# Query columns of the dilated attention units copied side by side on GpSimd

## The chip, the cores and the metric

One Trainium2 chip, one of its cores. The metric is the device time of one execution in microseconds. A core has five engines with queues of their own that work in order: TensorE (PE, matmuls, with its weight loads shown apart as PEld), VectorE (DVE), ScalarE (ACT), GpSimd (POOL) and SyncE (SP, which here only issues transfers).

## What is computed

One layer of a decoder trunk on x (2048 tokens, 1024 wide, float32): a norm, a projection, two token mixers side by side (a gated delta rule with four heads of 128, and a dilated sliding-window attention with eight heads of 64), an output projection, a norm, a gated MLP of width 2816 with a short convolution, and a last norm. The change lies in the dilated attention:

```python
DILATED_CONFIGS = ((128, 1), (512, 4), (2048, 16))      # window, dilation
for window, dilation in DILATED_CONFIGS:
    # tokens of equal residue modulo the dilation form a sequence of their own;
    # each of its blocks of 128 queries attends its own and the previous block
    sub = lambda t: t.reshape(bn, l, dilation, h, dh).transpose(0, 2, 3, 1, 4).reshape(bn * dilation, h, l, dh)
    o, lse = banded_causal_attention(sub(q), sub(k), sub(v), window // dilation, dilation, slopes)
    ...
weights = jax.nn.softmax(jnp.stack(lses), axis=0)
return jnp.einsum('gbsh,gbshd->bshd', weights, jnp.stack(outs))
```

## The kernel before

The program runs in stages: a projection (phase_p), the two mixers together (phase_mix, where gdn_rec is the delta rule and class Swa the attention), and the output projection and MLP (phase_e). phase_mix interleaves the steps of both mixers in one program; the framework's scheduler then fixes the order of each engine's queue before the program runs, and every wait is a semaphore.

An attention head has its queries and keys in SBUF with the features on the partitions and the 2048 tokens along the free dimension, as float32 split into two parts that PE takes at full rate: q2 holds both parts of q on 64 partitions each, k1 and k2 hold the two parts of k twice. load_qk brings the next head's three tiles while this one is worked on.

Swa.units lists 48 units of 128 queries in 19 groups: groups 0 to 7 are the near units (dilation 1, d = 0), groups 8 to 14 the 16 units of dilation 4 (d = 1; the four of group 8 have 128 keys, the other twelve 256, two units a group), groups 15 to 18 the 16 units of dilation 16 (d = 2, 128 keys, four units a group). Swa.cols (L563) takes a unit's columns from q2 or k1/k2: 128 or 256 neighbouring columns for d = 0, every fourth for d = 1, every sixteenth for d = 2. So the dilated units' columns lie 16 and 64 bytes apart.

Swa.scores (L600) goes through the groups. Each unit takes two products into one PSUM tile, q2 with k1 (L625) and q2 with k2 (L627); the query columns are the loaded weights, the key columns are streamed. VectorE then adds the bias and takes the row maximum (L632). At group 15 GpSimd spreads the maxima (spread, L664, L667), PE and VectorE gather them (L675, L677, L679), and after group 18 the common maximum of the three dilations goes back the same way.

Swa.values follows some 21 groups behind, so head h's values are worked on beside head h+1's scores: exponentials (L694), transposes on PE (L701), their copy by ScalarE (L704), the product with v (L722), and its sum into acc (L729, L735). Swa.divide (L740) is run in small steps beside the values of the next head: it stores the denominators, loads them reshaped, inverts and stores them, loads each quarter broadcast over 64 partitions (rb, L762, on SyncE's queue), multiplies on GpSimd (L769) and stores the quarter from ScalarE's queue (L771). The last head's division uses other buffers and engines. rb comes from a pool whose tiles have two buffers each unless told otherwise.

GpSimd's other work in this stage: block copies of the delta rule (L413, L414), its row scalings (L497 to L501), the attention's bias tiles (L548), and the spreading above.

Of the kernel before, what the change touches and what calls it, by code (L numbers as in the profile page):

```python
# [9 lines left out]
F32 = mybir.dt.float32  # L10
F32R = mybir.dt.float32r
# [7 lines left out]
P = 128  # L19
# [4 lines left out]
NB = T // 512  # L24
# [493 lines left out]
class Swa:  # L518
# [44 lines left out]
    def cols(self, t, d, u, prev, rows):  # L563
# [5 lines left out]
            return t[rows, :].rearrange("p (j r) -> p j r", r=4)[:, (u[0] + 1 - w) * P:(u[0] + 1) * P, u[1]]  # L569
        return t[rows, :].rearrange("p (j r) -> p j r", r=16)[:, :, u]  # L570

    def load_v(self, h):
        nc, n = self.n.nc, self.n
        src = n.sv[h // 4][T * (h % 4):T * (h % 4) + T, :]
        v = self.v[h % 2]
        nc.sync.dma_start(v[:, 32:48, :], src.rearrange("(p r) f -> p r f", r=16))
        for b in range(4):
            nc.sync.dma_start(v[:, 16 + 4 * b:20 + 4 * b, :],
                              src[512 * b:512 * b + 512, :].rearrange("(p r) f -> p r f", r=4))
        nc.sync.dma_start(v[:, 0:16, :], src.rearrange("(b p) f -> p b f", p=P))  # L580
# [19 lines left out]
    def scores(self, h):  # L600
        n = self.n
        nc, v = n.nc, n.nc.vector
        load = self.load_qk(h + 1, nc.sync, 2) if h + 1 < SH else iter(())
        q2, k1, k2 = self.loaded.pop(h)
        m = self.wk.tile([P, 48], F32, tag="m", name="m")
        nm = self.wk.tile([P, 48], F32, tag="nm", name="nm")
        mt = self.wk.tile([P, 32], F32, tag="mt", name="mt")
        tiles = []
        full = slice(0, P)
        for gi, (d, us) in enumerate(self.units()):  # L610
            if gi:
                next(load, None)
            if gi == 2 and h:
                self.slopes(h, (2,))
            if gi in (8, 15) and h + 1 < SH:
                self.slopes(h + 1, (gi // 15,))
            ps = n.bank(tag="sc")
            slot = self.free.pop(0)
            s = self.sp.tile([P, 512], F32, tag=f"s{slot}", name="s")
            o, rs = 0, []  # L620
            for col, u, prev in us:
                w = 256 if prev else P
                rs.append(slice(o, o + w))
                r = ps[:, o:o + w]
                nc.tensor.matmul(r, self.cols(q2, d, u, False, full), self.cols(k1, d, u, prev, full),  # L625
                                 start=True, stop=False)
                nc.tensor.matmul(r, self.cols(q2, d, u, False, full), self.cols(k2, d, u, prev, full),  # L627
                                 start=False, stop=True)
                o += w
            for (col, u, prev), r in zip(us, rs):  # L630
                bo = P if d < 2 and not prev else 0
                n.mark = v.tensor_tensor_reduce(out=s[:, r], in0=ps[:, r], in1=self.bias[d][:, bo:bo + r.stop - r.start], scale=1.0,  # L632
                                       scalar=-3e38, op0=ALU.add, op1=ALU.max, accum_out=m[:, col:col + 1])
            tiles.append((slot, s))
            if gi == 15:
                lay = self.spread(m[:, 0:32], 0)
            if gi == 17:
                self.gather(mt, lay, 0)
            yield None

        x = nm[:, 32:48]
        v.tensor_tensor(x, m[:, 32:48], mt[:, 0:16], op=ALU.max)
        v.tensor_tensor(x, x, mt[:, 16:32], op=ALU.max)
        v.tensor_scalar(x, x, -1.0, None, op0=ALU.mult)
        back = self.spread(x, 1)
        self.later = [lambda: self.gather(nm, back, 1)]
        yield tiles, nm
# [92 lines left out]
    def divide(self, h, acc):  # L740

        nc, v = self.n.nc, self.n.nc.vector
        n, last = self.n, h == SH - 1
        yield
        put, get = (nc.gpsimd, nc.gpsimd) if last else (nc.scalar, nc.sync)
        put.dma_start(n.den[h], acc[64:65, :])
        rd = self.wk.tile([P, 16], F32, tag="rd", name="rd")
        yield
        get.dma_start(rd, n.den[h].rearrange("o (p c) -> (o p) c", p=P))
        yield  # L750
        v.reciprocal(rd, rd)
        yield
        put.dma_start(n.rden[h].rearrange("o (p c) -> (o p) c", p=P), rd)
        yield
        rb = {}

        def load(b):
            if last:
                rb[b] = self.sp.tile([P, 512], F32, tag=f"s{b}", name="rbl")[0:64]
            else:  # L760
                rb[b] = self.wk.tile([64, 512], F32, tag="rb", name="rb")
            get.dma_start(rb[b], n.rden[h][:, 512 * b:512 * b + 512].to_broadcast([64, 512]))  # L762

        for b in range(4 if last else 2):
            load(b)
        yield
        for b in range(NB):
            c = slice(512 * b, 512 * b + 512)
            (v if last else nc.gpsimd).tensor_tensor(rb[b], rb[b], acc[0:64, c], op=ALU.mult)  # L769
            yield  # L770
            put.dma_start(n.ys[h // 2][64 * (h % 2):64 * (h % 2) + 64, c], rb[b])  # L771
            if b + 2 not in rb and b + 2 < NB:
                load(b + 2)
            yield

    def run(self):
# [660 lines left out]
```

## Time and profile before

| what | value |
|---|---|
| median of 3 runs | 2889.2 us (2887.18 to 2889.59) |
| the profiled execution's own time | 2890.9 us |
| its span in the profile | 2889.1 us |
| mean granted TensorE clock of the execution | 0.97 |
| PE busy, share of the span | 96% |
| DVE, ACT, POOL busy | 58%, 39%, 36% |
| mixers' stretch read below | 753 to 1250 us |

Busy times are those of one profiled execution. A matmul's start is recorded; its end is modelled, since matmuls are pipelined, so that a PE that is shown busy all the time can still be waiting inside its products for their weights or their streams. PEld is the weight load, which overlaps the matmul before it. [...]

### The profile page before, as it was taken

Reading aid. Unit: us, or ns where it says so; the run is one execution under the profiler, and the core shown is the slowest. Engines: PE = TensorE matmul, PEld = TensorE weight load, DVE = VectorE, ACT = ScalarE, POOL = GpSimd, SP = SyncE. Lnnn points to the kernel's source line nnn. Section 1 sums busy time; section 2 is a strip of 40 time slices with the busy share of each in tenths; the row PEclk is TensorE's granted clock in tenths of the full one; section 3 lists DMA queues with packets and bytes.
Section 4 is the critical chain, followed back from the end, with each engine's and each line's share of the span. In section 5 each row is a group of like instructions: output and inputs, shape, how many; then the busy total and the mean of one; then the engine's idle time right before and its main releaser. Section 6 shows DMA issues by size and latency. Waiting matters only on the chain.

```text
span 2889.1 us, 41075 instructions
## 1 busy us (share of the span) xinstructions
PE 2777.6 (96%) x14974; PEld 2344.6 (81%) x14974; DVE 1676.2 (58%) x2774; ACT 1122.1 (39%) x2349; POOL 1036.1 (36%) x1203
## 2 busy tenths in 40 slices
PE   8999999999999999989989889899999999999998
PEld 8998777777899999977877667687788887788887
DVE  5206455825555555544348767788777887654564
ACT  5313554342166555553234233333333333222233
POOL 4300322231112222211126666665665664412231
PEclk9999999999899998999999999999999999999999
DMA  5222343476766565336764454436333334875553
GB/s 181 83 60 98 114 132 125 125 212 181 219 162 174 158 164 149 102 88 196 222 203 139 133 171 144 131 101 224 110 110 108 100 93 134 296 245 181 177 196 133
DMA packets 369049, 438.70 MB, mean 152 GB/s; under 512 B 83991, under 2 KB 250183, under 8 KB 367431
## 3 DMA queue, kind: packets, MB, share of 16 engines
q1 hardware_dynamic: 321232, 406.76, 45.3%
q10 hardware_dynamic: 45390, 20.90, 2.7%
q0 software_dynamic: 2224, 8.42, 0.9%
q8 instruction: 118, 1.93, 0.3%
q14 instruction: 85, 0.70, 0.1%
HBM read 295.79 MB, written 140.18 MB: 151 GB/s over the span
## 4 chain that ended last, share of the span: by engine, by line
PE 38%; DMA 5%; POOL 4%; DVE 4%; issue 2%; SPq 1%; ACT 1%; POOLq 0%; DVEq 0%; ACTq 0%
PE tp L75 4%; PE tp L73 4%; PE tp L74 4%; PE sc L75 3%; PE sc L73 3%; PE sc L74 3%; PE g L75 3%; PE g L74 3%; PE g L73 3%; DMA sm<-hT 3%; PE pv L74 3%; PE pv L75 3%; PE pv L73 3%; POOL sm L1144 2%; DVE wl L68 1%
## 5 line engine op out<-in xcount | busy, mean ns | idle before, releaser
L68 DVE TENSOR_TENSOR wl<-wr,wh 128x512 fp32r<-128x512 f32 x220 | 270.4, 1259 | 38.3 <-ACT wh L67 37.4
L67 ACT CAST wh<-wr 128x512 fp32r<-128x512 f32 x220 | 135.7, 623 | 180.2 <-POOL wr L1102 54.5
L632 DVE CUSTOM_DVE_ANT_0 s<-sc,bias 128x256 f32<-128x256 f32 (+1 forms) x384 | 121.8, 363 | 124.6 <-PE sc L627 97.6
L1144 POOL TENSOR_TENSOR sm<-cv 128x512 f32<-128x512 f32 x110 | 179.1, 1657 | 35.7 <-issue 26.7
L67 ACT CAST ah<-ar 128x1408 fp32r<-128x1408 f32 x56 | 77.2, 1378 | 249.6 <-PE g L74 74.4
L1231 POOL TENSOR_TENSOR w<-w,w 128x512 f32<-128x512 f32 x55 | 90.6, 1666 | 229.3 <-DMA w<-in_w_down_dram 226.8
L73 PE MATMUL g<-hch,wh 128*128 128x512 f32 x352 | 145.3, 413 | 27.8 <-ACT g L1186 24.2
L722 PE MATMUL pv<-pt,sv 128*65 128x128 f32 x1200 | 171.2, 289 | 0.3
L73 PE MATMUL sc<-hch,wh 128*128 128x512 f32 x352 | 142.1, 404 | 16.4 <-ACT u L1186 15.6
L625 PE MATMUL sc<-k,q 128*128 128x256 f32 (+1 forms) x384 | 156.0, 413 | 1.1 <-DVE m L632 1.0
L694 ACT ACTIVATE s<-s,nm 128x256 f32<-128x256 f32 (+1 forms) x384 | 151.4, 460 | 9.2 <-POOL rb L769 4.7
L75 PE MATMUL g<-hch,wl 128*128 128x512 f32 x352 | 144.3, 410 | 6.3 <-DVE wl L68 6.3
L722 PEld LDWEIGHTS pv<-pt,sv 128*65 128x65 f32 x1200 | 146.5, 148 | 3.2 <-ACT pt L704 2.5
L74 PE MATMUL g<-hcl,wh 128*128 128x512 f32 x352 | 144.1, 409 | 0.0
L704 ACT COPY pt<-tp 128x512 f32<-128x512 f32 (+1 forms) x152 | 87.7, 578 | 142.7 <-PE tp L701 135.6
L627 PE MATMUL sc<-k,q 128*128 128x256 f32 (+1 forms) x384 | 142.3, 376 | 0.0
L75 PE MATMUL sc<-hch,wl 128*128 128x512 f32 x352 | 141.2, 401 | 0.4 <-DVE wl L68 0.4
L74 PE MATMUL sc<-hcl,wh 128*128 128x512 f32 x352 | 141.0, 401 | 0.0
L73 PE MATMUL tp<-hch,wh 128*128 128x512 f32 x352 | 139.3, 396 | 1.5 <-ACT wh L67 1.5
L75 PE MATMUL tp<-hch,wl 128*128 128x512 f32 x352 | 139.1, 395 | 0.0
L74 PE MATMUL tp<-hcl,wh 128*128 128x512 f32 x352 | 139.0, 395 | 0.0
L1124 DVE SCALAR_TENSOR_TENSOR cv<-g,fcw,cv 128x1024 f32<-128x1024 f32 x88 | 126.0, 1432 | 1.5
(374 smaller groups left out, 8117.6 us busy)
## 6 DMA issues: line engine op xcount, KB each, us to landing
ar<-act SPq DMA_DIRECT2D x56, 704.0 KB, 4.1
w<-in_w_down_dram SPq DMA_DIRECT2D x132, 256.0 KB, 5.3
act<-sm SPq DMA_DIRECT2D x110, 256.0 KB, 2.3
sm<-hT SPq DMA_DIRECT2D x92, 256.0 KB, 4.2
r<-in_w_gate_dram SPq DMA_DIRECT2D x66, 256.0 KB, 3.0
r<-in_w_up_dram SPq DMA_DIRECT2D x66, 256.0 KB, 4.1
xt<-in_x_dram SPq DMA_DIRECT2D x32, 512.0 KB, 3.7
zn<-zn SPq DMA_DIRECT2D x32, 512.0 KB, 5.5
```

What stands on the lines that cost most here:

```text
L67: (first or nc.scalar.copy)(hi, src)
L68: (e or nc.vector).tensor_tensor(lo, src, hi.bitcast(F32), op=ALU.subtract)
L73: nc.tensor.matmul(ps, ah, bh, start=start, stop=False, skip_group_check=more)
L74: nc.tensor.matmul(ps, ah, bl, start=False, stop=False, skip_group_check=more)
L75: nc.tensor.matmul(ps, al, bh, start=False, stop=stop, skip_group_check=more)
L625: nc.tensor.matmul(r, self.cols(q2, d, u, False, full), self.cols(k1, d, u, prev, full), start=True, stop=False)
L627: nc.tensor.matmul(r, self.cols(q2, d, u, False, full), self.cols(k2, d, u, prev, full), start=False, stop=True)
L632: n.mark = v.tensor_tensor_reduce(out=s[:, r], in0=ps[:, r], in1=self.bias[d][:, bo:bo + r.stop - r.start], scale=1.0, scalar=-3e38, op0=A ...
L694: nc.scalar.activation(s, s, AF.Exp, bias=nm[:, col:col + 1])
L722: nc.tensor.matmul(dst, self.vcols(h, d, u, back), pt[:, j * P:(j + 1) * P], start=(back == int(prev)), stop=(back == 0))
L1124: v.scalar_tensor_tensor(cv, g[:, j:j + 1024], self.cw[:, x, j:j + 1], cv, op0=ALU.mult, op1=ALU.add)
L1144: gp.tensor_tensor(src, x(*op_[0]), x(*op_[2]), op=ALU.add if op_[1] > 0 else ALU.subtract)
```

## The change

For the dilated units a new function, close, copies the query columns of two neighbouring units into a tile of two blocks of 128 contiguous columns (qc, three buffers), on GpSimd. A head has 16 such pairs; the first three copies are issued at group 6, each further one when a pair has been used up. The score products of the dilated units take their queries from these tiles; the keys are read as before, and so are the near units' queries. To make room, rb has one buffer in place of two: the division loads one quarter ahead of the first product and each later one after the store of the quarter before, with one step more between load and product.

```diff
--- before.py
+++ after.py
@@ -569,6 +569,17 @@
             return t[rows, :].rearrange("p (j r) -> p j r", r=4)[:, (u[0] + 1 - w) * P:(u[0] + 1) * P, u[1]]
         return t[rows, :].rearrange("p (j r) -> p j r", r=16)[:, :, u]
 
+    def close(self, q2, d, us):
+
+        t = self.wk.tile([P, 2, P], F32R, tag="qc", name="qc", bufs=3)
+        u = us[0][1]
+        if d == 1:
+            src = q2[:, 512 * u[0]:512 * u[0] + 512].rearrange("p (j r) -> p r j", r=4)[:, u[1]:u[1] + len(us)]
+        else:
+            src = q2.rearrange("p (j r) -> p r j", r=16)[:, u:u + len(us)]
+        self.n.nc.gpsimd.tensor_copy(t, src)
+        return t
+
     def load_v(self, h):
         nc, n = self.n.nc, self.n
         src = n.sv[h // 4][T * (h % 4):T * (h % 4) + T, :]
@@ -607,7 +618,12 @@
         mt = self.wk.tile([P, 32], F32, tag="mt", name="mt")
         tiles = []
         full = slice(0, P)
-        for gi, (d, us) in enumerate(self.units()):
+        units = self.units()
+        pairs = [(d, us[i:i + 2]) for d, us in units if d for i in range(0, len(us), 2)]
+        near = []
+        for gi, (d, us) in enumerate(units):
+            while pairs and len(near) < 3 and gi >= 6:
+                near.append(self.close(q2, *pairs.pop(0)))
             if gi:
                 next(load, None)
             if gi == 2 and h:
@@ -622,11 +638,14 @@
                 w = 256 if prev else P
                 rs.append(slice(o, o + w))
                 r = ps[:, o:o + w]
-                nc.tensor.matmul(r, self.cols(q2, d, u, False, full), self.cols(k1, d, u, prev, full),
-                                 start=True, stop=False)
-                nc.tensor.matmul(r, self.cols(q2, d, u, False, full), self.cols(k2, d, u, prev, full),
-                                 start=False, stop=True)
+                q = near[0][:, (len(rs) - 1) % 2] if d else self.cols(q2, d, u, False, full)
+                nc.tensor.matmul(r, q, self.cols(k1, d, u, prev, full), start=True, stop=False)
+                nc.tensor.matmul(r, q, self.cols(k2, d, u, prev, full), start=False, stop=True)
                 o += w
+                if d and len(rs) % 2 == 0:
+                    near.pop(0)
+                    if pairs:
+                        near.append(self.close(q2, *pairs.pop(0)))
             for (col, u, prev), r in zip(us, rs):
                 bo = P if d < 2 and not prev else 0
                 n.mark = v.tensor_tensor_reduce(out=s[:, r], in0=ps[:, r], in1=self.bias[d][:, bo:bo + r.stop - r.start], scale=1.0,
@@ -758,10 +777,10 @@
             if last:
                 rb[b] = self.sp.tile([P, 512], F32, tag=f"s{b}", name="rbl")[0:64]
             else:
-                rb[b] = self.wk.tile([64, 512], F32, tag="rb", name="rb")
+                rb[b] = self.wk.tile([64, 512], F32, tag="rb", name="rb", bufs=1)
             get.dma_start(rb[b], n.rden[h][:, 512 * b:512 * b + 512].to_broadcast([64, 512]))
 
-        for b in range(4 if last else 2):
+        for b in range(4 if last else 1):
             load(b)
         yield
         for b in range(NB):
@@ -769,8 +788,9 @@
             (v if last else nc.gpsimd).tensor_tensor(rb[b], rb[b], acc[0:64, c], op=ALU.mult)
             yield
             put.dma_start(n.ys[h // 2][64 * (h % 2):64 * (h % 2) + 64, c], rb[b])
-            if b + 2 not in rb and b + 2 < NB:
-                load(b + 2)
+            if b + 1 not in rb and b + 1 < NB:
+                load(b + 1)
+                yield
             yield
 
     def run(self):
```

## Rows read from the trace of the kernel before

**Rows 1.** Page, part 1: busy us, share of span and instructions of each engine.

```profile
PE 2777.6 (96%) x14974; PEld 2344.6 (81%) x14974; DVE 1676.2 (58%) x2774; ACT 1122.1 (39%) x2349; POOL 1036.1 (36%) x1203
```

**Rows 2.** Windows: stretch, length, busy PE, PEld, DVE, ACT, POOL, clock, DMA, GB/s.

```profile
753.00:1250.00 497.00, 492.39 (x4058) 470.37 (x4057) 271.52 (x1154) 261.63 (x692) 121.82 (x291) 0.92 0.58 156
895.90:914.00 18.10, 18.10 (x158) 17.28 (x156) 8.71 (x47) 2.80 (x6) 2.08 (x7) 0.91 0.11 24
914.00:930.00 16.00, 16.00 (x152) 15.55 (x150) 8.81 (x39) 14.09 (x44) 4.92 (x13) 1.00 1.07 251
```

**Rows 3.** Longest wait of PE, 753 to 1250 us: total us, times, longest.

```profile
PE g L424 <- DMA zn<-zn: 2.6, 1, 2.6
...
```

**Rows 4.** Timeline, near units: start us, length us, engine, line, operation.

```profile
755.69 0.19 PEld L625 LDWEIGHTS sc<-k,q 128*128 128x128 f32 x1
755.81 0.28 PE L625 MATMUL sc<-k,q 128*128 128x256 f32 x1
755.81 0.19 PEld L627 LDWEIGHTS sc<-k,q 128*128 128x128 f32 x1
```

**Rows 5.** Timeline, dilation 16, 128 keys; last, the load of what follows.

```profile
838.62 0.31 PEld L627 LDWEIGHTS sc<-k,q 128*128 128x128 f32 x1
838.84 0.31 PEld L625 LDWEIGHTS sc<-k,q 128*128 128x128 f32 x1
838.93 0.39 PE L625 MATMUL sc<-k,q 128*128 128x128 f32 x1
...
839.71 0.31 PEld L675 LDWEIGHTS tp<-sel,lay 128*128 128x128 f32 x1
```

**Rows 6.** Timeline, dilation 4, 128 keys.

```profile
1005.27 0.33 PEld L625 LDWEIGHTS sc<-k,q 128*128 128x128 f32 x1
1005.36 0.42 PE L625 MATMUL sc<-k,q 128*128 128x128 f32 x1
1005.50 0.33 PEld L627 LDWEIGHTS sc<-k,q 128*128 128x128 f32 x1
```

**Rows 7.** Timeline, dilation 4, 256 keys, from a group's first load on.

```profile
825.26 0.31 PEld L625 LDWEIGHTS sc<-k,q 128*128 128x128 f32 x1
825.47 0.33 PEld L627 LDWEIGHTS sc<-k,q 128*128 128x128 f32 x1
825.71 0.33 PEld L625 LDWEIGHTS sc<-k,q 128*128 128x128 f32 x1
825.92 0.42 PE L625 MATMUL sc<-k,q 128*128 128x256 f32 x1
```

**Rows 8.** Near units at the lower clock: their stretch in windows, two loads.

```profile
758.00:764.00 6.00, 4.53 (x31) 4.18 (x32) 1.81 (x9) 0.00 (x0) 0.00 (x0) 0.50 0.94 306
760.41 0.33 PEld L625 LDWEIGHTS sc<-k,q 128*128 128x128 f32 x1
760.62 0.33 PEld L627 LDWEIGHTS sc<-k,q 128*128 128x128 f32 x1
```

**Rows 9.** Groups of POOL, 753 to 1250 us: busy us, mean ns, idle before.

```profile
L769 POOL TENSOR_TENSOR rb<-rb,acc 64x512 f32<-64x512 f32 x24 | 30.2, 1272 | 55.8 <-DMA rb<-rden 53.0 <-issue 1.2 <-POOL ut L414 1.0
...
L548 POOL TENSOR_SCALAR bias<-dist 128x256 f32<-128x256 f32 x16 | 6.6, 414 | 31.6 <-DVE m L632 16.0 <-PE pv L75 15.3
```

**Rows 10.** Tile rb (issue ns, who waited, landing); SyncE's wait; window 1280 to 1290.

```profile
L762 SPq DMA_DIRECT2D rb<-rden x28: 444/450/1439, 875.7 to 1286.4; - x28
...
  ACT woh L67: 13.7, 1
...
DMA to landing us min/median/max: 2.3/3.1/5.1
...
SPq L762 <- DMA ys<-rb: 16.9, 10, 3.6
...
1280.00:1290.00 10.00, 5.29 (x41) 4.33 (x41) 2.56 (x3) 6.58 (x21) 4.63 (x6) 1.00 0.59 171
```

**Rows 11.** Waits of POOL, 753 to 1250 us: total us, times, longest.

```profile
POOL rb L769 <- DMA rb<-rden: 53.0, 12, 8.1
```

## The prediction

> **What bounds the kernel now.** I read the table of engines first: TensorE (PE) is busy for 2777.6 of 2889.1 us, no other engine above 58% [rows 1]. A busy share hides what a matmul waits inside itself, so I looked next at the stretch that the change touches, the mixer from 753 to 1250 us: PE 492.4 of 497 us, VectorE 271.5, ScalarE 261.6, GpSimd (POOL) 121.8, at a mean granted clock of 0.92 [rows 2]. The list of waits has only three of PE's there, and the longest is 2.6 us [rows 3]. So this stage ends when PE has issued its queue, and a change pays by what it takes out of PE's issue time.
>
> What a score product costs PE is read from the timeline, in starts, not in durations (ends of matmuls are modelled). Each product is a weight load of 128 query columns and a matmul that streams 128 or 256 key columns. My reading: a load starts when the matmul before it has taken over its own weights, and a matmul's start stands where the stream before it ended. Then load to next load is what one product costs, and load to its own matmul's start is the key stream of the product before. Near units (queries and keys contiguous): loads 0.12 us apart, 256 keys streamed in 0.12 [rows 4]. Units of dilation 16 (both operands strided by 16 elements, 128 keys): from 838.62 to 839.71 five products, 0.218 us each, while the matmul starts 0.09 after its load [rows 5]. Dilation 4 with 128 keys: 0.23 apart, stream 0.09 [rows 6]. Dilation 4 with 256 keys: 0.24 apart, stream 0.21 [rows 7]. Twice the keys at the same stride cost the same, and the stream of 128 is done in less than half the interval: so the strided query load, about 0.22 to 0.24 us against at most 0.12 contiguous, sets the price wherever 128 keys are streamed. With 256 strided keys the stream is nearly as long as the load and will be left over.
>
> [...]
>
> **The change part by part.** *Contiguous queries for PE.* A head has 16 units of dilation 4 (4 with 128 keys, 12 with 256) and 16 of dilation 16, two products each, over 8 heads: 256 products of dilation 16, 64 and 192 of dilation 4. After the change a product costs the longer of a contiguous load (0.115, the middle of what [rows 4] allow) and the key stream before it.
> - Dilation 16: 256 x (0.218 - 0.115) = 26.4 us.
> - Dilation 4, 128 keys: 64 x (0.23 - 0.115) = 7.4 us.
> - Dilation 4, 256 keys, second to fourth product of a group: the stream of 0.21 stays. Two decimals make the gain 0.02 to 0.03; 144 x 0.025 = 3.6 us.
> - The first of each group of four follows a short stream and costs 0.21 now, as the first two loads show [rows 7]: 48 x (0.21 - 0.115) = 4.6 us.
>
> Sum 42.0 us. [...] 42.0 x 0.84 = 35.3 us. The clock falls in the very stretch in which dilation 16 is scored (0.91 in 895.9 to 914) [rows 2]. Denser products there could keep it up; I count none of that in the sum, but in the range.
>
> *The copies.* 8 + 8 pairs per head, 128 copies of 128x256 on POOL. No copy with strided reads is in the trace. From below: the one-input 128x256 operation of L548, 0.414 us [rows 9]. From above: the two-input product of L769, 1.272 us for 512 elements, so 0.64 for 256 [rows 9]. I take 0.45, nearer the one-input row since the copy has one input: 58 us (53 to 82). POOL has 375 us free in the stage, so that lies beside other work; it goes from 25% to 36% busy.
> [...]
>
> *The new wait.* The first load of a pair now waits for its copy, and a copy waits until PE is through with the pair three places before (three buffers). The copies run three pairs ahead: three groups at dilation 4, one and a half at dilation 16. A head's 19 groups take some 62 us (497 / 8), so 3.3 us a group, and the lead is 5 to 10 us against a copy of half a microsecond. Behind a copy that waits for PE stand POOL's block copies, scalings, bias and spreading steps (L413, L414, L497 to L501, L548, L664, L667) and the division's product (L769); PE and VectorE wait for those, all with a step or more in between. I cost this at 0. If that cover is gone it is the first rival.
>
> *One buffer for the division.* rb goes from two buffers to one. Each of seven heads now does product, store on ScalarE's queue, load on SyncE's queue, four times in a row: 1.27 us, 0.45 of issue, 2.3 or more of landing, 0.45 of issue, 3.1 of landing [rows 9, 10]: 7.6 us a turn, three turns in series against about one before, and a turn has three steps of 3.3 us. Of SyncE's loads three per head wait for a store instead of two; such waits took 16.9 us over ten times [rows 10], so at most some 12 us more, before loads that are issued a head or several steps ahead. Covered in the middle of the stage, where PE's waits for a DMA were 2.6 us. Not covered for head 6, whose division runs after the last scores: there ScalarE already waited 13.7 us for L769 and PE was busy for 5.29 of 10 us [rows 10]. The two further turns cost between 0 and 15 us; I take 3, because these turns also have steps between them, though shorter ones.
>
> Sum: 35.3 - 3 = 32 us. From this execution's 2890.9 us (span 2889.1 and 1.8 around it): 2859. The median of the runs shown, 2889.2, lies 1.7 below it: **2857 us**.
>
> **The rivals.**
> *POOL's queue holds PE (slower).* POOL works in order. Its product L769 stood for 53.0 us, in 12 waits of up to 8.1, for its broadcast to land [rows 9, 11]; until now nothing urgent stood behind. Now copies do, and with one buffer each of 28 products can wait. It decides when a wait outlasts the lead of 5 us at dilation 16. If each of the 28 held PE for 2 us: 56 us lost against 32 won, 2889.2 + 24 = 2913. The turning point is 1.2 us each. Against it: 8.1 is the longest, the mean of the twelve is 4.4, below the lead.
> *The keys set the price.* Strided keys stay. If they, not the load, make the 0.218, the change gains only in the first of each group, 4.6 x 0.84 = 3.9, less the 3 of the division: 2888. For it: 0.21 of stream in [rows 7]; against it: the 0.09 of [rows 5, 6].
> *The next engine catches part.* ScalarE is busy for 14.1 of 16 us just after dilation 16 [rows 2]. If half of what PE saves turns into waits there, 35.3 / 2 - 3 = 15: 2874.
> [...]
>
> **How the numbers follow.** Forecast 0.46, clock 0.15, next engine 0.20, keys 0.08, POOL's queue 0.11. The range reaches from 2836 (clock, with a little more) to 2886: it leaves out POOL's queue, most of the keys and the ends of the others, under 0.2. Bounds of the unknown costs (division 0 to 15 us: 2854 to 2869) are inside. A difference below about 0.2%, 5.8 us, is no more than a measurement of this kernel can tell. Faster by more: forecast, clock and next engine, 0.80. Same: keys and a sliver, 0.09. Slower: 0.11.
>
> **What would show it.** Right: loads of dilation 16 some 0.11 apart and of dilation 4 with 256 keys some 0.21, the stretch of dilation 16 some 3 us shorter per head, copies of 0.4 to 0.65 us, no rows of PE waiting for POOL's copies. Wrong: dilation 16 still near 0.218 (keys); PE's waits naming the copies (queue); products close together but PE idle before ScalarE's tiles (next engine); the granted clock of the stage above 0.96 (clock). The prediction fails most simply if the strided copy takes several times the 0.64 us bound.

## The result, and the profile after

| what | before | after |
|---|---|---|
| median | 2888.19 us (4 runs) | 2857.87 us (4 runs) |
| ratio, 95% interval | | 0.988 (0.9862 to 0.9899) |
| profiled execution, its span | 2890.9, 2889.1 us | 2855.64, 2853.9 us |
| first to last weight load of the score products, in the profile | 493.7 us | 461.8 us |

The forecast was 2857 us with a range of 2836 to 2886. The total was met almost exactly, but it was met by a sum whose terms moved against each other, and that is what most of the runs are about. The two medians alone give 0.9895, a difference of 30.3 us; the 0.988 is the ratio on record with its interval, which holds both. The two profiled executions lie further apart than the medians, 35.2 us in their spans.

The engines' table of the page after answers to [rows 1]; the window of the mixers' stretch, 29 us shorter, answers to [rows 2]: PE is no longer busy throughout (451 of 468 us, idle for 17.0 where it was idle for 4.6), GpSimd went from 122 to 201 us, the mean granted clock from 0.92 to 0.95.

```profile
PE 2731.5 (96%) x14974; PEld 2290.8 (80%) x14974; DVE 1679.3 (59%) x2774; ACT 1119.4 (39%) x2349; POOL 1107.6 (39%) x1331
```

```profile
752.00:1220.00 468.00, 450.98 (x4077) 419.82 (x4076) 275.18 (x1155) 260.88 (x696) 200.94 (x423) 0.95 0.61 167
```

The timeline of the kernel after, first three loads and one matmul of dilation 16 (against [rows 5]), then one whole group of dilation 4 with 256 keys and the load that follows it (against [rows 7]). Columns: start, length, engine, line, operation.

```profile
895.15 0.19 PEld L642 LDWEIGHTS sc<-k,qc 128*128 128x128 f32 x1
895.22 0.29 PE L642 MATMUL sc<-k,qc 128*128 128x128 f32 x1
895.26 0.19 PEld L643 LDWEIGHTS sc<-k,qc 128*128 128x128 f32 x1
895.37 0.19 PEld L642 LDWEIGHTS sc<-k,qc 128*128 128x128 f32 x1
...
876.33 0.19 PEld L642 LDWEIGHTS sc<-k,qc 128*128 128x128 f32 x1
876.44 0.19 PEld L643 LDWEIGHTS sc<-k,qc 128*128 128x128 f32 x1
876.65 0.21 PEld L642 LDWEIGHTS sc<-k,qc 128*128 128x128 f32 x1
876.88 0.21 PEld L643 LDWEIGHTS sc<-k,qc 128*128 128x128 f32 x1
877.12 0.21 PEld L470 LDWEIGHTS g<-ri,ut 128*128 128x128 f32 x1
```

A product of dilation 16 now takes 0.11 us, half of [rows 5], and its load 0.19 where it was 0.31. In the 256-key group the first product takes 0.11, the second 0.21, the others 0.23: only the first is really cheaper than in [rows 7].

GpSimd's copies in the stretch after (busy us, mean ns, idle before), against the bounds from [rows 9]:

```profile
L580 POOL CAST qc<-q 128x256 fp32r<-128x256 f32 x128 | 79.8, 640 | 106.5 <-PE sc L643 103.1 <-issue 2.9
```

A copy takes 640 ns, at the upper of the two bounds and not near the lower. Before the copies GpSimd is idle for 103 us until PE has given a buffer back: on the whole the copies are early, and GpSimd waits for PE far more than PE for it. The waits of PE, ScalarE and SyncE in that stretch (total us, times, longest), against [rows 3, 10]:

```profile
PE pv L741 <- ACT pt L723: 4.9, 7, 1.8
PE sc L642 <- POOL qc L580: 3.7, 7, 1.0
...
ACT s L713 <- POOL rb L788: 24.7, 9, 4.2
ACT pt L723 <- POOL qc L580: 11.7, 3, 4.4
ACT pt L723 <- POOL rb L788: 5.4, 1, 5.4
...
SPq L781 <- DMA ys<-rb: 76.9, 18, 6.2
```

In the kernel before ScalarE's waits for the product, 753 to 1250 us, were:

```profile
ACT s L694 <- POOL rb L769: 4.7, 3, 2.7
ACT pt L704 <- POOL rb L769: 4.0, 1, 4.0
```

Three things are new. PE waits for copies, a little. ScalarE stands for 42 us in front of work of GpSimd, 8.7 before: between two of its own tiles lies a store of the division that needs the rb product, and ScalarE's queue is in order. (The three waits put down to a copy, L580, stand behind such a store too: it is issued within 0.04 us of the product's end.) And SyncE stands for 77 us before it may load the single rb buffer again, against 16.9 in [rows 10].

Where the time went, from my own sum over the two traces (each weight load's start to the next one's, from the first score product to the load behind the last, in us):

```
                          before    after
near units                  43.6     43.4
dilation 4, 128 keys        16.4      9.8
dilation 4, 256 keys        47.9     40.9
dilation 16                 60.0     43.6
everything else of PE      326.0    324.2
sum                        493.9    462.0
of it at the lower clock    80.5     46.5
```

(The lower clock by the loads' starts; the trace's own record of the granted clock, which has only 1.00 and 0.50 in both, has 81.9 and 47.6 us.) 30.0 of 31.9 us are the dilated products themselves. The other 2.4 us of the span's 35.2 lie behind the stretch, and the stretch begins 1 us earlier.

### The profile page after: what moved, and what is told of

Its sections match the earlier page's. It is cut to its first block, busy times and chain, and to the rows that moved or that the text cites. A ratio compares the mean times of both kernels' runs of the same rounds, so it can differ in the third digit from the quotient of the medians.

```text
span 2853.9 us, 41288 instructions
## 1 busy us (share of the span) xinstructions
PE 2731.5 (96%) x14974; PEld 2290.8 (80%) x14974; DVE 1679.3 (59%) x2774; ACT 1119.4 (39%) x2349; POOL 1107.6 (39%) x1331
## 4 chain that ended last, share of the span: by engine, by line
PE 74%; DMA 7%; POOL 6%; DVE 5%; issue 4%; ACT 3%; SPq 1%; ACTq 0%; POOLq 0%; DVEq 0%
PE tp L75 6%; PE tp L73 6%; PE tp L74 6%; PE sc L75 5%; PE sc L73 5%; PE sc L74 5%; PE pv L74 5%; PE pv L75 5%; PE pv L73 5%; PE g L75 4%; PE g L73 4%; PE g L74 4%; DMA sm<-hT 3%; PE pv L741 2%; POOL sm L1164 2%
## 5 line engine op out<-in xcount | busy, mean ns | idle before, releaser
L651 DVE CUSTOM_DVE_ANT_0 s<-sc,bias 128x256 f32<-128x256 f32 (+1 forms) x384 | 121.5, 361 | 105.2 <-PE sc L643 87.4
L741 PE MATMUL pv<-pt,sv 128*65 128x128 f32 x1200 | 162.6, 279 | 5.3 <-ACT pt L723 4.9
L741 PEld LDWEIGHTS pv<-pt,sv 128*65 128x65 f32 x1200 | 137.7, 141 | 10.3 <-ACT pt L723 9.4
L580 POOL CAST qc<-q 128x256 fp32r<-128x256 f32 x128 | 79.8, 640 | 106.5 <-PE sc L643 103.1
```

Of the source, the lines that this page charges most:

```text
L741: nc.tensor.matmul(dst, self.vcols(h, d, u, back), pt[:, j * P:(j + 1) * P], start=(back == int(prev)), stop=(back == 0))
```

## The experiments

Two theories were to be told apart first. Mine: the strided query load set the price of a dilated product, the copies and the division cost next to nothing. The rivals: the keys, the clock or a changed order brought the gain, or the copies and the single buffer cost a good part of a larger one. All ratios are to the kernel before, run on the same chip as the experiment; medians of different chips are not compared. Sums over traces are set side by side across chips.

### The division's part alone

```diff
-                rb[b] = self.wk.tile([64, 512], F32, tag="rb", name="rb")
+                rb[b] = self.wk.tile([64, 512], F32, tag="rb", name="rb", bufs=1)
-        for b in range(4 if last else 2):
+        for b in range(4 if last else 1):
...
```

> The kernel before with the division's part alone: one rb buffer, one load ahead, one more step; queries stay strided, no copies. My theory (the gain is the contiguous query load; the division costs 0 to 3 us): 2888 to 2892 us. Rival (single buffer is dear, and the copies win more than the total shows): 2900 or more, with SyncE's waits for the stores of rb above 60 us and PE waiting for ScalarE. Rival (the gain comes from the changed order around the division): 2875 or less.

Measured: ratio 0.9991 (0.9977 to 1.0006); the score stretch of its trace 493.5 us against 493.7. Nothing is gained by the order around the division, and by itself the single buffer costs nothing that can be measured, not even the 3 us that I had put down.

### The copies made and not used

```diff
-                q = near[0][:, (len(rs) - 1) % 2] if d else self.cols(q2, d, u, False, full)
+                q = self.cols(q2, d, u, False, full)
```

> The changed kernel with all 128 copies made but not used: the products of the dilated units read q2 strided as before. My theory (copies lie beside other work): product intervals 0.218 and 0.235 as before, 2888 to 2894 us in all. Rival (the copies themselves hold other engines through GpSimd's queue): 2900 or more. Rival (what gained was a changed order or clock, not the contiguous load): below 2875.

Measured: ratio 1.0039 (1.0023 to 1.0054), some 11 us slower. The dilated products cost what they did before (17.3, 48.1 and 60.1 us by the sum above), so the gain of the change is in the contiguous load and in nothing else that came with it. But the copies were not free. Waits of GpSimd, VectorE and PE, 753 to 1270 us:

```profile
POOL qc L580 <- DMA q<-sq: 39.2, 10, 7.5
...
DVE oo L506 <- POOL so L501: 16.3, 4, 4.5
...
PE g L441 <- DVE q L433: 10.5, 5, 4.4
```

Here no reader gives a buffer back, so the copies run ahead until they stand before a tile of queries that has not landed, and then come one after the other, with the rest of GpSimd's queue behind and between them. Its row scalings (L501) come late, VectorE stands for them (L506), and PE stands for the copy that follows in VectorE's queue (L433). The same mechanism as in my first rival, by another wait; in the changed kernel PE's buffers keep the copies back and this wait is not among GpSimd's longest. The queue need not be the whole of the 11 us: in this trace the score stretch ran for 113 us at the lower clock, against 82 before, and the profiled execution took 7 us more than the median. How the two divide is not shown.

### No copies, contiguous columns

```diff
+    def near(self, q2, d, u):
+        c = u if d == 0 else 4 * u[0] + u[1] if d == 1 else u
+        return q2[:, c * P:(c + 1) * P]
...
-                q = near[0][:, (len(rs) - 1) % 2] if d else self.cols(q2, d, u, False, full)
+                q = self.near(q2, d, u)
...
```

> The changed kernel without any copy: the dilated units take 128 neighbouring columns of q2 directly as their queries, which are other queries than theirs, so the scores are of other tokens; all instructions of PE, their shapes and the keys are the same. My theory: dilation 16 at 0.11 between loads, dilation 4 with 256 keys at 0.11, 0.21, 0.233, 0.233, and none of the 6 us in which PE's loads waited for copies, less of ScalarE's waits: 2848 to 2854 us. Rival (copies and their waits are wholly hidden): 2857 to 2859. Rival (the copies' order had helped): 2862 or more.

Measured: ratio 0.987 (0.9844 to 0.9895), against 0.988 of the changed kernel: within the intervals the same. In its trace dilation 16 takes 38.0 us where the changed kernel's takes 43.6, so the waits for copies cost PE some 6 us there. The whole score stretch is 8 us shorter than the changed kernel's (453.6 against 461.8). The profiled span is shorter by less than 1 us only because what lies behind the last value product took 7.5 us more; beside this run the kernel before, too, took some 6 us more than beside the changed kernel (2894.5 against 2888.2). So the total neither shows nor excludes a cost of the copies of this size.

### Contiguous keys too

```diff
+    def plain(self, t, d, u, prev):
+        c = 4 * u[0] + u[1] if d == 1 else u
+        return t[:, (c - prev) * P:(c + 1) * P]
...
-                nc.tensor.matmul(r, q, self.cols(k1, d, u, prev, full), start=True, stop=False)
-                nc.tensor.matmul(r, q, self.cols(k2, d, u, prev, full), start=False, stop=True)
+                nc.tensor.matmul(r, q, self.plain(k1, d, u, prev), start=True, stop=False)
+                nc.tensor.matmul(r, q, self.plain(k2, d, u, prev), start=False, stop=True)
```

> The changed kernel with the dilated units' keys also read as neighbouring columns (other keys than theirs, so the scores are of other tokens); copies and all shapes as in the changed kernel. My theory (with 256 keys the strided key stream, 0.233 us, sets what is left): intervals of dilation 4 with 256 keys fall to about 0.12, 144 of them by 0.11 and what follows a group by 0.12 in 48 places, 20 us at most: 2838 to 2846 us; dilation 16 stays at 0.11, since there the contiguous load is the longer. Rival (something else than the key stream holds the 256-key products): intervals stay at 0.21 to 0.233 and the time at 2858.

Measured: ratio 0.9881 (0.9855 to 0.9907). The timeline of a 256-key group and the load after it:

```profile
878.82 0.19 PEld L646 LDWEIGHTS sc<-k,qc 128*128 128x128 f32 x1
878.92 0.19 PEld L647 LDWEIGHTS sc<-k,qc 128*128 128x128 f32 x1
879.04 0.19 PEld L646 LDWEIGHTS sc<-k,qc 128*128 128x128 f32 x1
879.16 0.19 PEld L647 LDWEIGHTS sc<-k,qc 128*128 128x128 f32 x1
879.28 0.64 PEld L470 LDWEIGHTS g<-ri,ut 128*128 128x128 f32 x5
```

The theory on the key stream holds: 0.12 us where the changed kernel has 0.21 and 0.23. The time it was to bring did not come. PE had 13.6 us less to do in these groups (27.3 against 40.9) and the stretch was no shorter (467.6 us against 461.8, in an execution that took 8 us more than the median). Two things can have taken the gain. One is the clock: the stretch ran for 78 us at the lower level, 48 in the changed kernel, and the mean granted clock of the four executions was 0.970 to 0.973, against 0.974 to 0.977. The other is that PE's issue time is not the only bound any more; the waits, 753 to 1230 us, say where to look for that:

```profile
PE pv L745 <- ACT pt L727: 17.4, 14, 2.5
...
ACT s L717 <- POOL rb L792: 24.3, 9, 4.1
```

### The stores of the division moved from ScalarE's queue to SyncE's

```diff
-        put, get = (nc.gpsimd, nc.gpsimd) if last else (nc.scalar, nc.sync)
+        put, get = (nc.gpsimd, nc.gpsimd) if last else (nc.sync, nc.sync)
```

The changed kernel was run again beside it as the yardstick.

> The changed kernel once more, as the yardstick on the chip on which the next three run: ratio to the kernel before 0.986 to 0.990.

> The changed kernel with the division's stores (den, rden and the quarters of y) of heads 0 to 6 issued from SyncE's queue in place of ScalarE's. In the changed kernel ScalarE stands about 30 us for the rb product before such a store, against 9 before. Theory A (PE's queue is no longer the only bound; part of what it saved is lost behind ScalarE's queue): ScalarE's waits for the rb product gone, stage shorter, 4 to 12 us faster than the changed kernel. Theory B (PE is still the bound, ScalarE's waits lie beside its work): within 3 us of the changed kernel. Theory C (SyncE, held by the store, delays loads that PE needs): slower by 5 us or more, with PE waiting for DMAs.

Measured: the changed kernel 2860.97 us, ratio 0.989 (0.9871 to 0.9909); with the stores moved 2842.99 us, ratio 0.9823 (0.9804 to 0.9843). 18 us for one line, more than theory A had asked. ScalarE's longest waits in the stretch are then all for PE, the first two:

```profile
ACT pt L723 <- PE tp L720: 121.1, 51, 4.6
ACT wi L471 <- PE g L470: 46.8, 13, 33.7
```

PE's wait for ScalarE's tiles is down to 1.5 us, the score stretch to 449.4 us, and the values after the last score product take 48.3 us instead of 52.6. SyncE now stands 64.6 us before the product instead of ScalarE, and nobody waits for that.

### The same move in the kernel before

> The kernel before with the division's stores on SyncE's queue and nothing else changed. Theory A (before the change PE was the bound, so ScalarE's waits of some 10 us lay beside its work): ratio 0.998 to 1.001. Theory B (the stores held the stage in both kernels): ratio 0.994 or less, as the 18 us that the same edit gave the changed kernel.

Measured: ratio 0.9956 (0.9941 to 0.997), 13 us faster; neither theory's number. From the last score load to the last value product the profile has 48.0 us against 56.7 in the kernel before; the score stretch is 487.7 against 493.7 us, with 63 us at the lower clock against 82. So my reading that the stage ended when PE had issued its queue was too strict already for the kernel before: the tail behind the scores was not PE's alone. For the stretch itself it is not refuted, since 19 us less at the lower clock can account for the 6 us (in the kernel before a near product took 0.119 us at the full clock and 0.213 at the lower, medians).

With ScalarE free in both, the change is worth 0.9823 / 0.9956 = 0.987, some 38 us, against 31 without (0.989 on the same chip as the 0.9823). That some 7 us of what PE saved had been lost behind ScalarE's queue is likely by the waits, but the intervals are wide enough to leave it open.

### One dilation at a time

```diff
-        pairs = [(d, us[i:i + 2]) for d, us in units if d for i in range(0, len(us), 2)]
+        pairs = [(d, us[i:i + 2]) for d, us in units if d == 2 for i in range(0, len(us), 2)]
...
```

> The changed kernel with copies for dilation 16 alone; dilation 4 takes strided queries as before. By the sums of the two traces dilation 16 gave 16.5 of 30.0 us of product time, dilation 4 with 128 keys 6.6, with 256 keys 7.0. Theory A (a saved product counts fully): 13 us slower than the changed kernel. Theory B (GpSimd's copies cost in waits, and the 48 copies of the 256-key groups give back little): 3 to 8 us slower. If dilation 4 gives nothing at all: same as the changed kernel.

> The changed kernel with copies for dilation 4 alone; dilation 16 takes strided queries as before. Theory A (saved product time counts fully): 16 us slower than the changed kernel, ratio about 0.994. Theory B (dilation 4 gives back little more than its 64 copies cost): ratio 0.998 or more.

Measured: dilation 16 alone 0.9911 (0.9894 to 0.9929), 26 us, 5.5 us short of the changed kernel; dilation 4 alone 0.9942 (0.9928 to 0.9956), 17 us. For dilation 16 alone theory B gives the number, for dilation 4 alone theory A. Each gives more than its own products (18.3 and 13.6 us by the sums of their traces); together they give 31, not 43. The lower clock goes along with it: 82 us of the stretch before, 61 and 65 with one dilation, 48 with both, so the second half finds less left to win. Another part may be what ScalarE's queue keeps; by the runs with moved stores that is some 7 us, as far as they tell. How the 12 us divide between the two is not shown.

### Contiguous keys with the stores moved

> The kernel with neighbouring key columns for the dilated units (other keys than theirs, so the scores are of other tokens), whose products were 13.5 us shorter without any gain in the total, now with the division's stores on SyncE's queue. Theory A (ScalarE's queue, held by the rb product, had taken the place of PE): 8 to 20 us faster than with the stores on ScalarE's queue, 0.980 to 0.984 of the kernel before. Theory B (something else, the chain of the maxima or the clock, holds it): 0.986 to 0.990 as there.

Measured: ratio 0.9852 (0.9828 to 0.9876), between the numbers of the two theories. It is some 8 us faster than with the stores on ScalarE's queue, but the two intervals overlap, and it is not faster than the kernel with strided keys and moved stores (0.9823). So that ScalarE's queue was one part of why shorter products brought nothing is not shown by these two runs. The clock is the part that shows: in the profiled execution the score stretch ran for 95 us at the lower level, against 37.5 us in the kernel with strided keys and moved stores, and dilation 16 took 55.2 us, 24.4 of them at the lower level. That execution took 12 us more than the median, but the mean granted clock of all five lies at 0.968 to 0.975, against 0.976 to 0.980. Why the clock falls more there was not tried and stays open.

### No copies, with the stores moved

> The kernel without copies (neighbouring columns of q2 as the dilated units' queries, so the scores are of other tokens), with the division's stores on SyncE's queue. It gives what the copies cost in all once ScalarE is free. Theory A (copies hidden but for PE's short waits for them): 0 to 6 us less than the changed kernel with its stores moved (ratio 0.980 to 0.9823). Theory B (the copies cost as they did where they were made and not used, 11 us): ratio 0.978 or less.

Measured: ratio 0.9795 (0.978 to 0.981). Against 0.9823 with the 128 copies that is 0.28%, 8 us, the intervals just touching: this is the best figure for what the copies cost, and the score stretches of the two traces, 438.5 and 449.4 us, point the same way. Theory A named 0 to 6, theory B 11.

### Fewer copies

```diff
+        pairs = []
+        for d, us in units:
+            if d == 1 and us[0][2]:
+                if us[0][1][1] == 0:
+                    pairs.append((1, [us[0], (0, (us[0][1][0], 2), True)]))
+            elif d:
+                pairs += [(d, us[i:i + 2]) for i in range(0, len(us), 2)]
...
+                wide = d == 1 and prev
+                if wide:
+                    q = self.cols(q2, d, u, False, full) if u[1] % 2 else near[0][:, u[1] // 2]
...
```

> The changed kernel with the division's stores on SyncE's queue and with only the first unit of each 256-key group copied (one copy per block holds the first units of its two groups; the second unit takes strided queries, since the stream of 256 strided keys, 0.233 us, is as long as the strided load): 104 copies in place of 128. Theory A (a strided load hidden behind that stream costs nothing): the intervals of a 256-key group stay at 0.11, 0.21, 0.235, 0.235 and the time is within 3 us of the kernel with only the stores moved, or up to 4 us less if GpSimd's queue had cost. Theory B (loads and stream get in each other's way): 4 us or more slower.

Measured: 2837.24 us, ratio 0.9793 (0.9779 to 0.9806), the best of all and as good as no copies at all. Against 0.9823 with 128 copies it is some 9 us less, more than theory A had asked, with the intervals just touching; against the 0.988 and 0.989 of the change itself, 25 to 28 us. The loads of a 256-key group stand 0.110, 0.211, 0.237 and 0.237 apart: a strided load behind a strided stream of 256 keys costs 4 ns. PE's waits for copies in the stretch are down to one row:

```profile
PE sc L652 <- POOL qc L580: 1.1, 2, 0.6
```

## Why the prediction was right, point by point

- **The mechanism.** Right. Loads 0.11 apart for dilation 16, 0.11 and 0.21 for the first two of a 256-key group; the run with contiguous keys shows that the key stream, and the one with unused copies that the query load, set what I said they set. The rival of the keys is out for dilation 16 and true for three of four products with 256 keys, where I had counted it.
- **Dilation 16.** Mis-sized. 26.4 us by the rows, 22 after the factor 0.84 for the clock; the trace has 16.5. A product is at 0.112 us, as forecast, but 5.6 us (43.6 against the 38.0 without copies) are new waits: the load of the second pair of groups 16 and 17 stands 0.3 to 1.3 us behind the load before it in about half of the heads, where 0.11 was due. The step that failed is "I cost this at 0": the lead of one and a half groups was long enough on the mean, and not when other work of GpSimd stood in front of the copy. At group 16 that is the row scalings, the spreading and the bias of the same step. At group 17, in four heads and for some 3 us in all, it is the division's product, in three of the four after a wait for its broadcast: the first rival, on a small scale. Head 2 shows it, GpSimd first, then the load that waits for the copy:

```profile
896.48 1.26 POOL L788 TENSOR_TENSOR rb<-rb,acc 64x512 f32<-64x512 f32 x1 [2.48 <-DMA rb<-rden]
897.70 1.29 POOL L580 CAST qc<-q 128x256 fp32r<-128x256 f32 x2
...
898.41 0.19 PEld L642 LDWEIGHTS sc<-k,qc 128*128 128x128 f32 x1 [0.77 <-POOL qc L580]
```

- **Dilation 4.** 128 keys: 6.6 us against 7.4, or 6.2 after the clock. 256 keys: 7.0 against 8.2, or 6.9 after the clock, but not in the places where I had put it: the first of a group gives 0.10, the second 0.02, the third and fourth next to nothing, since the strided stream takes 0.233 and not the 0.21 that I had read from the matmul's start.
- **The clock.** No run shows the factor 0.84 of the sum; it was my estimate. In its place the two traces show 80.5 of 493.9 us at the lower clock before and 46.5 of 462.0 after, and there the contiguous load gained next to nothing: a product of dilation 16 took 0.217 us before and 0.213 after, against 0.217 and 0.112 at the full clock (medians). The factor took the time at the lower clock as given, and it fell. The rest of PE's work shows both sides: 302 of its loads stood at the lower clock before, 157 after (52.3 to 22.0 us), while at the full clock its loads went from 92 to 97 ns on the mean, with 13.5 us more in intervals of over 0.4 us (1.9 before, 15.4 after). The sum of the two is the 1.8 us of the table. The clock is not a matter of one profile: the eight executions of the changed kernel had a mean granted clock of 0.974 to 0.977, those of the kernel before that stand beside the experiments 0.966 to 0.974. A clock that stays up longer, which I counted in the range alone, and the rival "next engine" both came true in part and cancelled.
- **The copies.** 0.64 us, not 0.45, so 80 us of GpSimd and not 58. The upper bound, half of L769's 1.272 us, was the better one; the row that I chose as nearest, L548 with 0.414 us, reads contiguous columns. Their cost is some 8 us in all, not 0. VectorE's score work is not slowed by them (L651 takes 421 ns, L632 before 422); only one of its groups, L506, went from 370 to 480 ns. A slip of the sum: the turning point of the first rival is 32 / 28 = 1.1 us, not 1.2.
- **The division.** 3 us, from 0 to 15: by itself nothing, and the tail was not longer (53.0 us from the last score load to the last value product, 56.7 before). The term rested in part on a misread row. The 13.7 us of [rows 10] are not a wait for head 6: ScalarE stood there for VectorE's product of the last head, which the change leaves as it was.

```profile
ACT woh L67 <- DVE rbl L769: 13.7, 1, 13.7
```

SyncE's wait for the stores grew by 60 us (76.9 against 16.9), not by 12. That did not cost PE directly, but the stores hold ScalarE for 42 us in the stretch where it was some 9, and this is where the runs with moved stores put some 7 us of the gain, within their noise.
- **The bound.** The statement that PE's queue alone ends the stage was too strong: with the stores moved the changed kernel is 18 us faster without any work taken from PE, and the tail of the kernel before gets shorter too.

So 2857 came out of a sum in which the products gave less than I counted (30.0 for 35.3) and the division took nothing. In the two profiles the rest of the span gave another 5 us, which the medians, 30.3 us apart, do not show. The direction and the size were right for the stated reason; that it fits to 1 us is luck.

## What to carry to other kernels

Read a matmul's price from the starts of its weight load, its matmul and the next load: here that split it into what the load and what the stream set (0.218 us a product of dilation 16 before, of which the stream took 0.09), and it said in advance which of the two set the price. It did not say what the total gains: contiguous keys made the products of the 256-key groups shorter, as read from the rows (27.3 us against 40.9), and the kernel no faster (0.9881 against 0.988). Before a saving on a saturated engine is counted, look for an in-order queue next to it that already waits for something slow, however little: taking one engine's stores out of its queue gave 13 us before the change and 18 us after it. Copy only those operands whose load is not hidden behind a longer stream: 104 copies in place of 128 gave some 9 us.

## What the hardware showed

- A weight load of 128 columns at the full clock, from load to load: 0.112 us contiguous (dilation 16, kernel after), 0.217 with one column every 64 bytes (dilation 16, kernel before), 0.233 with one every 16 bytes (dilation 4 with 128 keys, kernel before): here the wider stride was the cheaper one. A stream of 256 columns of the split float32: 0.119 contiguous (near units, both kernels), 0.233 with one column every 16 bytes (dilation 4, kernel after); of float32 that is not split, contiguous, 0.215 (L352, kernel before).
- Both ran beside each other: a strided load behind a strided stream cost 0.237 (the run with fewer copies) where the stream alone took 0.233.
- Contiguous keys went along with more time at the lower clock: 95 us of the score stretch, 37.5 us with strided keys, in the two profiles with moved stores.
